# K blocks of 3, 3, 3, 3 and 4 chunks instead of four of 4 in the first layer's input projection

## The chip, the cores and the metric

The kernel runs on one core of one Trainium2 chip. The metric is the device time of one execution in microseconds, the median of three runs.

## The reference

A decoder trunk of two layers on 256 tokens of width 2048. Each layer has a mixer and a gated feed-forward part, each behind an RMS norm whose scale and shift come from a conditioning vector `c`. Cut to what the change touches:

```python
c_act = jax.nn.silu(c)
for l in range(DEPTH):
    mod = c_act @ w_mod[l] + b_mod[l]
    shift1, scale1, gate1, shift2, scale2, gate2 = jnp.split(mod[:, None, :], 6, axis=-1)
    h = rms_norm(x, norm1_gain[l]) * (1.0 + scale1) + shift1
    x = x + gate1 * hybrid_token_mixer(h, ...)      # proj = h @ w_in[l], then three mixers, then @ w_out[l]
    h = rms_norm(x, norm2_gain[l]) * (1.0 + scale2) + shift2
    x = x + gate2 * swiglu_ffn(h, ...)
return rms_norm(x, final_norm_gain)
```

All is float32. `w_mod[l]` is 2048 x 12288, and most of `w_in[l]` (3336 columns of it) is multiplied in the stage that the change touches.

## The kernel before, in words

**Engines.** TensorE (PE) does the products, VectorE (DVE) and ScalarE (ACT) the work around them, GpSimd (POOL) small fills, and the SyncE queue (SP) issues all transfers in order. A scheduler lays out each engine's order at build time from the order in which the code is written and from its own idea of durations; at run time every engine goes through its list in order.

**Modulation.** `mod = c_act @ w_mod` is done on DVE, not on PE. `mod_segment(l, part, k0, nk)` makes the `nk` chunks (128 columns each) from `k0` on of one part. A chunk row of `w_mod` comes in by DMA (L220) and L223 adds it, times one value of `c_act`, to an accumulator: 16 steps for the 16 chunks of `c`. Then `finish` transposes the accumulator on PE into the one `fin` bank (L248), DVE sums each column over the partitions (L250), and L253 (shift) or L256 (scale) writes the columns that the norm uses. In layer 0 a shift and a scale segment of a block run side by side, their steps in turn, in 128x512 buffers `g`.

**Pacing.** All steps stand in one list `mods`. The projection calls `tick` after each job, which pops steps at a rate; what is still missing when a norm asks for its columns is done there by `need`:

```python
rate[0] += rate[1] * weight          # weight: columns of the job / 1024
...
if mods and mods[0][0] not in closed:
    mods.popleft()[1]()
```

The rate is 3.3 in layer 0 and 1.6 in its last block. The segments of the gate and of the second norm are `closed` until the last block starts; their steps are 1024 wide, in two buffers `mraw`.

**The projection of layer 0.** It goes in K blocks. For each block, `norm` scales `x` (L441), transposes it (L444), applies scale and shift (L447 on ACT) and rounds (L450, L451); then four groups of columns are projected, "qk" (1024), "z" (520), "v" (768) and "bq" (1024). A job is one chunk of K of one group: a weight tile (L323), in one of nine buffers named `raw`, `wh` and `wl`, and float32 products (L358) with the two row blocks of 128 tokens into four `acc` banks. Behind the last job of a group the banks are evacuated: in the first block ACT copies them (L967), in the others DVE adds them to what stands there (L969). The normalised chunks lie in tiles of four chunks:

```python
j, i0 = divmod(at, 4)
n = min(4 - i0, ks[-1] + 1 - at)
if j not in res:
    res[j] = (tl_h32(), *(tl(hmp, [P, 4, P], "hm", F32R) for _ in range(2)))
```

Layer 1 takes all 16 chunks in one block, and the list of blocks is used nowhere else but here:

```python
for n in K_BLOCKS:
    for pair in zip(*(mod_segment(0, part, k0, n) for part in (SHIFT1, SCALE1))):
        mods.extend(pair)
    k0 += n
```

Of the kernel before, what the change touches and what calls it, by code (L numbers as in the profile page):

```python
# [33 lines left out]
FAR = 1.0e30  # L34


K_BLOCKS = (4, 4, 4, 4)
TAIL_OUT = (3, 6)
TAIL_FFN = (3, 5)
LEAD_FFN = (0, 0)  # L40
# [63 lines left out]
def trunk(ctx: ExitStack, tc, x, cT, pos, small, consts, b_mod, w_mod, w_in, w_gk, w_out,  # L104
# [369 lines left out]
    k0 = 0  # L474
    for n in K_BLOCKS:
        for pair in zip(*(mod_segment(0, part, k0, n) for part in (SHIFT1, SCALE1))):
# [472 lines left out]
    def layer(l):  # L949
        wi, wo = w_in[l], w_out[l]  # L950
        load_small(l)
        blocks, at = [], 0
        for n in (K_BLOCKS if l == 0 else (KD,)):
            blocks.append(range(at, at + n))
# [263 lines left out]
```

## Time and profile before

| | us |
|---|---|
| median of three runs | 2579.19 (2578.09 to 2586.53) |
| profiled execution | 2585.34 |
| its span, first to last instruction | 2583.5 |
| PE busy in the span | 2432.7 |
| DVE busy in the span | 1714.4 |
| first L358 matmul starts | 40.83 |
| layer 0's first norm has its columns | 40.19 |

Rows of the profile give an engine, a line, what is written from what, shapes and a count. In the order of time the first two columns are the start and the length in us, and a bracket at the end tells how long the engine stood idle ahead of the row and whose end it waited for. PE's ends are modelled, and merged rows overlap a little at their ends.

### The profile page before, as it was taken

How to read it: one execution, taken by the hardware profiler on the slowest of the kernel's cores; microseconds unless marked ns; L12 is line 12 of the kernel's file. 1: busy time of each engine (PE TensorE's matmuls, PEld its weight loads, DVE VectorE, ACT ScalarE, POOL GpSimd, SP SyncE). 2: the span in 40 equal slices, each digit the busy share in tenths (PEclk: the TensorE clock that was granted, in tenths of full speed). 3: DMA queues.
4: the chain of work that ended last, by engine and by line, in shares of the span. 5: the costliest groups of instructions: out<-in, count | busy, mean ns of one | idle time of the engine just before them, and what ended most of it. 6: DMA issues, size and time to landing. Idle time of an engine off the chain costs nothing.

```text
span 2583.5 us, 30803 instructions
## 1 busy us (share of the span) xinstructions
PE 2432.7 (94%) x11164; PEld 1884.1 (73%) x11164; DVE 1714.4 (66%) x2171; ACT 1053.5 (41%) x1548; POOL 58.2 (2%) x117
## 2 busy tenths in 40 slices
PE   4999998889999988999999999999999999999998
PEld 2555785447878767788877878877778878888876
DVE  6767867576675777657578785888664575544555
ACT  2203443124444333344335454564644434344443
POOL 1000000000000000000000000000000000000000
PEclk9999999989999999999999999999999999999999
DMA  9996538777778888868687861675676686666654
GB/s 341 368 322 204 180 114 282 258 231 268 261 259 260 283 268 274 292 193 286 223 277 261 281 192 50 214 232 192 212 256 193 200 286 195 188 191 188 189 184 155
DMA packets 190033, 600.79 MB, mean 233 GB/s; under 512 B 21628, under 2 KB 26268, under 8 KB 189496
## 3 DMA queue, kind: packets, MB, share of 16 engines
q1 hardware_dynamic: 189880, 598.81, 70.7%
q8 instruction: 88, 1.44, 0.2%
q14 instruction: 65, 0.53, 0.1%
HBM read 596.63 MB, written 2.10 MB: 232 GB/s over the span
## 4 chain that ended last, share of the span: by engine, by line
PE 57%; DMA 20%; DVE 10%; issue 8%; ACT 4%; POOL 1%; SPq 1%; DVEq 0%; ACTq 0%; POOLq 0%
PE acc L358 48%; DMA mraw<-in_w_mod 13%; DVE wl L331 4%; DMA raw<-in_w_down 3%; DMA raw<-in_w_in 2%; DVE acc L223 2%; ACT wh L330 1%; PE mm L403 1%; PE ga L895 1%; DMA raw<-in_w_up 1%; PE mm L678 1%; PE mm L685 1%; PE ga L916 1%; DMA raw<-in_w_gate 1%; PE fin L248 1%
## 5 line engine op out<-in xcount | busy, mean ns | idle before, releaser
L358 PE MATMUL acc<-wh,hm 128*128 128x512 f32 (+3 forms) x4872 | 1339.2, 389 | 20.9 <-DVE xs L931 4.7
L330 ACT ACTIVATE wh<-raw 128x1024 fp32r<-128x1024 f32 (+3 forms) x669 | 684.7, 1025 | 985.8 <-PE acc L358 548.9
L331 DVE TENSOR_TENSOR wl<-raw,wh 128x1024 fp32r<-128x1024 f32 (+3 forms) x669 | 785.2, 1179 | 446.6 <-ACT wh L330 444.5
L358 PEld LDWEIGHTS acc<-wh,hm 128*128 128x128 f32 x4872 | 892.0, 189 | 215.8 <-issue 25.5
L358 PE MATMUL acc<-wl,hm 128*128 128x512 f32 (+3 forms) x2484 | 792.3, 394 | 12.2 <-DVE wl L331 9.7
L223 DVE SCALAR_TENSOR_TENSOR acc<-mraw,c_act,acc 128x1024 f32<-128x1024 f32 x320 | 410.3, 1282 | 225.2 <-DMA mraw<-in_w_mod 222.9
L358 PEld LDWEIGHTS acc<-wl,hm 128*128 128x128 f32 x2484 | 458.4, 190 | 124.1 <-DVE wl L331 22.3
L358 PE MATMUL acc<-wh,ahl 128*128 128x512 f32 x560 | 158.4, 397 | 0.0
L358 PEld LDWEIGHTS acc<-wh,ahl 128*128 128x128 f32 x560 | 105.8, 189 | 24.5
L358 PE MATMUL acc<-wl,ahl 128*128 128x512 f32 x280 | 90.8, 398 | 7.2 <-DVE wl L331 7.2
L223 DVE SCALAR_TENSOR_TENSOR g<-g,c_act,g 128x512 f32<-128x512 f32 x128 | 88.7, 747 | 12.6 <-DMA g<-in_w_mod 12.4
L358 PE MATMUL acc<-wh,b 128*128 128x512 f32 (+2 forms) x184 | 74.7, 545 | 2.2 <-ACT b L447 2.1
L358 PE MATMUL acc<-wl,b 128*128 128x512 f32 (+2 forms) x176 | 67.1, 518 | 2.6 <-DVE g L969 2.6
L358 PEld LDWEIGHTS acc<-wl,ahl 128*128 128x128 f32 x280 | 52.2, 189 | 23.1 <-DVE wl L331 11.3
L358 PE MATMUL acc<-raw,b 128*128 128x512 f32 (+2 forms) x176 | 67.6, 524 | 0.0
L358 PEld LDWEIGHTS acc<-wh,b 128*128 128x128 f32 x184 | 35.2, 197 | 30.8 <-issue 23.1
L358 PEld LDWEIGHTS acc<-wl,b 128*128 128x128 f32 x176 | 32.8, 192 | 29.2 <-issue 20.3
L416 ACT ACTIVATE acc<-xs 128x512 f32<-128x512 f32 x32 | 19.0, 595 | 85.7 <-DVE xs L931 85.7
L447 ACT ACTIVATE b<-mm,mod,mod 128x128 f32<-128x128 f32 x24 | 9.2, 461 | 109.7 <-DVE mod L256 92.1
L358 PEld LDWEIGHTS acc<-raw,b 128*128 128x128 f32 x176 | 33.5, 195 | 26.7 <-issue 21.7
L929 DVE TENSOR_TENSOR acc<-acc,gate 128x512 f32<-128x512 f32 x64 | 43.0, 695 | 10.3 <-PE acc L358 10.2
L358 PE MATMUL acc<-raw,hm 128*128 128x512 f32 x88 | 41.7, 598 | 1.4 <-ACT acc L416 1.4
(314 smaller groups left out, 1645.8 us busy)
## 6 DMA issues: line engine op xcount, KB each, us to landing
mraw<-in_w_mod SPq DMA_DIRECT2D x320, 512.0 KB
raw<-in_w_down SPq DMA_DIRECT2D x176, 512.0 KB
raw<-in_w_gate SPq DMA_DIRECT2D x160, 512.0 KB
raw<-in_w_up SPq DMA_DIRECT2D x160, 512.0 KB
raw<-in_w_in SPq DMA_DIRECT2D x72, 512.0 KB
g<-in_w_mod SPq DMA_DIRECT2D x128, 256.0 KB
raw<-in_w_out SPq DMA_DIRECT2D x43, 512.0 KB
raw<-in_w_in SPq DMA_DIRECT2D x32, 264.0 KB
```

Of the source, the lines that this page charges most:

```text
L223: V.scalar_tensor_tensor(acc, raw[:, a], c_act[:, i + a:i + a + 1], acc, ALU.mult, ALU.add)
L248: TE.transpose(ps[:, i * P:(i + 1) * P], acc[:, (j + i) * P:(j + i + 1) * P], ident)
L330: A.activation(wh[:, :width], raw[:, :width], AF.Copy)
L331: V.tensor_tensor(wl[:, :width], raw[:, :width], wh[:, :width].bitcast(F32), ALU.subtract)
L358: TE.matmul(ps[blk, j][:, :segs[j][2]], xa, parts[j][part], start=i == 0 and n == 0, stop=last and n == len(terms) - 1)
L403: TE.transpose(ps[:, j * P:(j + 1) * P], src[:, j * P:(j + 1) * P], ident)
L416: A.activation(scr[0]() if junk is None else junk, xs[:, blk, j * 512:(j + 1) * 512], AF.Square, accum_out=ssq[blk][:, j:j + 1])
L678: TE.matmul(ps[:, s], LT[blk][:, s], Tm[blk][:, s], start=True, stop=True)
L685: TE.matmul(ps[:, s], U[blk][:, s], m1[:, s], start=True, stop=True)
L895: TE.matmul(ps[:, j * nk:(j + 1) * nk], qT[rows, i + j], kT[rows, g, :nk], start=True, stop=True)
L916: TE.matmul(ps[:, j * 64:(j + 1) * 64], pT[:, j * nk + kb * P:j * nk + (kb + 1) * P], kv[kb][:, P + g * 64:P + (g + 1) * 64], start=kb == ...
L929: V.tensor_tensor(ps, ps, need(gate_row, (l, part, j)), ALU.mult)
```

## The change

```diff
-K_BLOCKS = (4, 4, 4, 4)
+K_BLOCKS = (3, 3, 3, 3, 4)
```

Blocks now start at chunks 0, 3, 6, 9 and 12. The first four pairs of segments are 384 columns wide instead of 512, and there are 160 steps of them in all instead of 128. A block that does not start at a multiple of four is normalised in up to two pieces, so the norm runs in 7 pieces for each row block instead of 4. There is one more round of evacuations.

The rate of steps stays as it is: 3.3 times 3.258 (the columns of one chunk over 1024) is 10.75 steps for a chunk, 43 for a block of four and 32.25 for a block of three; each next pair of segments has 32 steps.

PE at the end of the first block, before: the last jobs of "bq" (`acc_560` to `acc_565`), the finish of the next block's two segments (`fin`), a transpose of the norm, and the second block's first job (`acc_690` on).

```order
L358 MATMUL acc_565<-wl_583,b_331 128x512
L248 MATMUL fin_640<-consts_88,g_357 128x128 x4
L358 MATMUL acc_560<-raw_601,b_195 128x512
L358 MATMUL acc_565<-raw_601,b_331 128x512
L248 MATMUL fin_649<-consts_88,g_363 128x128 x4
L358 MATMUL acc_560<-wh_616,b_195 128x512
L358 MATMUL acc_565<-wh_616,b_331 128x512
L444 MATMUL mm_677<-consts_88,b_675 128x128 x4
L358 MATMUL acc_690<-wl_688,b_656 128x512
```

(The two middle matmuls of each job are left out.) The same place now:

```order
L358 MATMUL acc_518<-raw_546,b_327 128x512
L358 MATMUL acc_519<-raw_546,b_327 128x512
L248 MATMUL fin_574<-consts_88,g_351 128x128 x3
L248 MATMUL fin_582<-consts_88,g_357 128x128 x3
L358 MATMUL acc_624<-wh_622,b_195 128x512
L444 MATMUL mm_605<-consts_88,b_603 128x128
L444 MATMUL ga_615<-consts_88,b_613 128x128 x2
L358 MATMUL acc_625<-wh_622,b_195 128x512
L358 MATMUL acc_628<-wh_622,b_327 128x512
```

Both `fin` groups have moved from between the last jobs of a block to behind its last matmul, and the next block's first matmul follows them.

DVE at the end of the second block, before: the evacuations of "bq" (L969) among steps of the fourth block's segments; the third block's columns were written some 25 rows earlier.

```order
L223 SCALAR_TENSOR_TENSOR g_828<-g_963,c_act_102,g_828 128x512
L969 TENSOR_TENSOR b_151<-b_151,acc_885 128x512
L969 TENSOR_TENSOR b_153<-b_153,acc_886 128x512
L969 TENSOR_TENSOR b_163<-b_163,acc_889 128x512
L223 SCALAR_TENSOR_TENSOR g_841<-g_966,c_act_102,g_841 128x512
L969 TENSOR_TENSOR b_165<-b_165,acc_890 128x512
L223 SCALAR_TENSOR_TENSOR g_828<-g_969,c_act_102,g_828 128x512
```

The same place now, with the third block's columns (`sums`, `mod`) behind the last evacuation and steps of the fourth block's segments (`g_897`, `g_903`) between them:

```order
L969 TENSOR_TENSOR b_163<-b_163,acc_783 128x512
L223 SCALAR_TENSOR_TENSOR g_897<-g_900,c_act_102,g_897 128x384
L969 TENSOR_TENSOR b_165<-b_165,acc_784 128x512
L250 TENSOR_REDUCE sums_251_839<-fin_840 128x3
L223 SCALAR_TENSOR_TENSOR g_903<-g_906,c_act_102,g_903 128x384
L253 COPY mod_6_3_250_838<-sums_251_839 128x3
L250 TENSOR_REDUCE sums_254_847<-fin_848 128x3
L223 SCALAR_TENSOR_TENSOR g_897<-g_909,c_act_102,g_897 128x384
L256 SCALAR_TENSOR_TENSOR mod_6_3_253_846<-sums_254_847,gains_131 128x3
```

What has moved is the finish of the next block's segments, from a place inside the block to its end. At the end of the fourth block, DVE's last step of the scale segment and a 1024-wide step of the gate stand there as well:

```order
L223 SCALAR_TENSOR_TENSOR g_1146<-g_1341,c_act_102,g_1146 128x512
L969 TENSOR_TENSOR b_165<-b_165,acc_1301 128x512
L223 SCALAR_TENSOR_TENSOR g_1152<-g_1344,c_act_102,g_1152 128x512
L250 TENSOR_REDUCE sums_408_1358<-fin_1359 128x4
L253 COPY mod_12_4_407_1357<-sums_408_1358 128x4
L250 TENSOR_REDUCE sums_411_1367<-fin_1368 128x4
L223 SCALAR_TENSOR_TENSOR acc_1407<-mraw_1410,c_act_102,acc_1407 128x1024
L256 SCALAR_TENSOR_TENSOR mod_12_4_410_1366<-sums_411_1367,gains_131 128x4
```

The gate's first step stood ahead of the last block's start by a group and more before (in row with the third block's "v" evacuations); it now stands in the finish itself.

## The prediction

> **What bounds the kernel now.** I read the page first, then busy time by stage, then the waits and the order of time of the first 220 us, where the change lies.
>
> ```profile
> span 2583.5 us, 30803 instructions
> PE 2432.7 (94%) x11164; PEld 1884.1 (73%) x11164; DVE 1714.4 (66%) x2171; ACT 1053.5 (41%) x1548; POOL 58.2 (2%) x117
> ```
>
> TensorE is busy 94% of the span. Busy time in two stretches (columns: stretch, length, then busy us of PE, PEld, DVE, ACT, POOL, then granted clock, DMA share, GB/s), and all that PE waited for from 84 to 198 us:
>
> ```profile
> 0.00:40.00 40.00, 3.35 (x12) 2.14 (x12) 26.74 (x57) 11.19 (x25) 6.59 (x27) 1.00 0.92 325
> 40.00:200.00 160.00, 157.31 (x468) 84.77 (x468) 109.50 (x175) 25.99 (x59) 2.73 (x16) 1.00 0.97 344
> PE fin L248 <- DVE sums L250: 0.8, 1, 0.8
> ```
>
> So there are 40 us in which PE has next to nothing, then 160 us in which it is the bound, although DMA is at 0.97 too. The three old block borders lie in the second stretch: the second block's last group gives way to the third's first at 138.59 us, and the third's ends with transposes at 184.59, both without a wait:
>
> ```profile
> 138.59 3.67 PE L358 MATMUL acc<-raw,b 128*128 128x512 f32 x8
> 184.59 0.60 PE L444 MATMUL mm<-consts,b 128*128 128x128 f32 x4
> ```
>
> A chunk of K is thus (184.59 - 138.59) / 4 = 11.5 us of PE. What the change can win is in the first 40 us, and what it can lose is at the borders. Order of time at the start, DVE then PE:
>
> ```profile
> 26.89 9.56 DVE L223 SCALAR_TENSOR_TENSOR g<-g,c_act,g 128x512 f32<-128x512 f32 x14 [0.38 <-DMA g<-in_w_mod]
> 36.88 0.69 DVE L250 TENSOR_REDUCE sums<-fin 128x4 f32<-128x512 f32 x1 [0.42 <-PE fin L248]
> 38.78 0.69 DVE L250 TENSOR_REDUCE sums<-fin 128x4 f32<-128x512 f32 x1 [1.00 <-PE fin L248]
> 39.38 0.74 DVE L223 SCALAR_TENSOR_TENSOR g<-g,c_act,g 128x512 f32<-128x512 f32 x1
> 40.04 0.15 DVE L256 SCALAR_TENSOR_TENSOR mod<-sums,gains 128x4 f32<-128x4 f32 x1
> ...
> 35.72 1.12 PE L248 MATMUL fin<-consts,g 128*128 128x128 f32 x4 [16.02 <-DVE g L223]
> 37.62 1.12 PE L248 MATMUL fin<-consts,g 128*128 128x128 f32 x4 [0.78 <-DVE sums L250]
> 40.83 2.08 PE L358 MATMUL acc<-wh,b 128*128 128x512 f32 x2 [2.09 <-ACT b L447]
> ```
>
> This is the finish chain of a modulation segment: transposes into the one `fin` bank, reduce, second transposes, second reduce, the scale column, ACT's L447, the first matmul. From the first `fin` at 35.72 to the matmul at 40.83 it takes 5.1 us. Its multiply-adds run back to back, 9.56 us for 14, 0.68 each: DVE sets the start, with DMA close behind (one 0.38 us gap).
>
> **The change part by part. The start.** A multiply-add on 384 instead of 512 columns is priced from two widths, and DMA's pace from the busiest row:
>
> ```profile
> L223 DVE SCALAR_TENSOR_TENSOR g<-g,c_act,g 128x512 f32<-128x512 f32 x60 | 41.7, 745 | 3.6 <-DMA g<-in_w_mod 3.6
> L223 DVE SCALAR_TENSOR_TENSOR acc<-mraw,c_act,acc 128x1024 f32<-128x1024 f32 x11 | 14.1, 1283 | 12.2 <-DMA mraw<-in_w_mod 12.2
> ...
> 20.00:40.00 20.00, 2.23 (x8) 1.43 (x8) 18.13 (x28) 0.00 (x0) 1.05 (x2) 1.00 1.00 361
> ```
>
> (1283 - 745) / 512 = 1.05 ns a column, so 128 columns fewer save 0.134 us, and the 32 of the first block 4.3 us. The chain loses two transposes (0.28 each, from 1.12 for four) and two times 0.13 of reduce, 0.8 together. The next transposes now stand ahead of the first matmul instead of behind it, worth nothing either way, and the slow first matmuls (2.08 for two) stay. Sum: -5.1. Lower bound -4 (DMA becomes the limit with its shorter rows), upper -7 (DMA sheds 2.1 MB, 5.8 us at 361 GB/s of the 20 to 40 us row, and DVE's gaps go too).
>
> **The borders.** A block needs 32 multiply-add steps for the next block's columns. The pace is 3.3 steps per 1024 columns of projection, 10.75 a chunk. Four chunks gave 43, so steps ran ahead; three give 32.25, so a block's last step now stands at the very end of the block before it. The order on PE shows it: before, both `fin` groups stand inside the last output group, ahead of its last jobs; now they stand behind its last matmul, at all four borders, and the next matmul needs their columns. So the finish chain, hidden until now behind bq matmuls, is exposed four times. How it ran when covered, and how DVE drains a group (PE, then DVE, near a border):
>
> ```profile
> 86.14 0.60 PE L248 MATMUL fin<-consts,g 128*128 128x128 f32 x4
> 86.58 3.60 PE L358 MATMUL acc<-wh,b 128*128 128x512 f32 x8
> 90.45 3.60 PE L358 MATMUL acc<-wl,b 128*128 128x512 f32 x8
> ...
> 137.93 0.69 DVE L969 TENSOR_TENSOR b<-b,acc 128x512 f32<-128x512 f32 x1 [0.17 <-PE acc L358]
> 138.53 0.74 DVE L223 SCALAR_TENSOR_TENSOR g<-g,c_act,g 128x512 f32<-128x512 f32 x1
> 139.19 0.68 DVE L969 TENSOR_TENSOR b<-b,acc 128x512 f32<-128x512 f32 x1
> ```
>
> I lay out each border from T, the end of the last bq matmul, with these pitches: `fin` of three warm 0.4, reduce 0.55, evacuation 0.6, multiply-add 0.54 (384) or 0.68 (512), scale column to first matmul 0.8 (40.04 to 40.83).
> - First border (the old block's evacuations are ACT's): fin 0.5, reduce to 1.1, fin and a multiply-add to 1.75, reduce to 2.3, matmul at 3.1.
> - Second: the last evacuation waits behind a multiply-add and ends at 0.95; reduce 1.5, multiply-add 2.0, second reduce 2.65, multiply-add 3.2, matmul at 4.0.
> - Third: the same with 512-wide multiply-adds: 4.6.
> - Fourth: the last scale step itself stands behind the last evacuation (1.75), two 4-wide reduces to 3.6, then a 1024-wide multiply-add (1.2) ahead of the column: 5.6.
>
> Together 17.3 us. PE does 39 transposes in there (0.11 each, from 0.43 for four) that it did elsewhere before: 4.3. Net +13.0; between 11 (multiply-adds between the reduces slip) and 15 (0.1 us more for each hand-over).
>
> **The clock.** What a stall of that size does afterwards is seen at 199 us, when PE waited for an evacuation:
>
> ```profile
> 201.50 2.20 PE L358 MATMUL acc<-wl,b 128*128 128x260 f32 x6 [2.58 <-DVE g L969]
> 206.10 1.19 PE L358 MATMUL acc<-raw,b 128*128 128x260 f32 x4
> ...
> 199.00:200.00 1.00, 0.00 (x0) 0.00 (x0) 0.43 (x1) 0.00 (x0) 0.00 (x0) 1.00 0.83 291
> 203.00:204.00 1.00, 1.00 (x4) 0.74 (x3) 1.00 (x2) 0.00 (x0) 0.00 (x0) 0.50 0.98 389
> 205.00:206.00 1.00, 1.00 (x4) 0.81 (x3) 0.92 (x1) 0.00 (x0) 0.00 (x0) 0.50 1.04 348
> 206.00:207.00 1.00, 1.00 (x5) 0.82 (x5) 0.37 (x1) 0.00 (x0) 0.00 (x0) 0.81 0.94 377
> ```
>
> 2.58 us of idling, and the granted clock stood at 0.50 from 203 to about 206.2 us: 3.2 us at half speed, 1.6 lost. A 0.78 us wait at 115 us did not lower it:
>
> ```profile
> 115.74 0.55 PE L248 MATMUL fin<-consts,g 128*128 128x128 f32 x3 [0.78 <-DVE sums L250]
> 116.00:117.00 1.00, 1.00 (x6) 0.52 (x5) 1.00 (x4) 0.00 (x0) 0.00 (x0) 1.00 1.07 403
> ```
>
> Idle time without the transposes is 2.4, 3.0, 2.8 and 4.7 us at the four borders, so each is nearer to the first case: four times 1.6, less a little chance of escape, +6. Ends: 1.6 (only the fourth) and 8.
>
> [...]
>
> **The last block.** The gate stream's first step and its nineteenth, and DVE's load behind them:
>
> ```profile
> 170.54 1.28 DVE L223 SCALAR_TENSOR_TENSOR acc<-mraw,c_act,acc 128x1024 f32<-128x1024 f32 x1
> 223.50 1.28 DVE L223 SCALAR_TENSOR_TENSOR acc<-mraw,c_act,acc 128x1024 f32<-128x1024 f32 x1
> ...
> 220.00:240.00 20.00, 19.94 (x65) 9.87 (x64) 19.55 (x50) 9.90 (x16) 1.16 (x2) 1.00 0.68 242
> ```
>
> Before, its first evacuations stood behind the eleventh step of the gate stream, which began at 170.5 us, 14 us ahead of the block; that made the 2.58 us stall and its 1.6 to 2 us of slow clock. Now the stream begins at the border and the evacuations stand behind its sixth step. The steps came one per 2.9 us (18 intervals from 170.54 to 223.50), so the sixth ends near T + 4.8 + 5 x 2.9 = 19.3; the evacuation is wanted near T + 18.4 (5.6, four jobs of 3.44, 1.6 of slow clock, less the last 2.6). I take half of the old 4.6 us as won back: -2.3 (0 to -4.6).
>
> Five stream steps are thereby pushed to DVE behind the block, 5 x 1.28 = 6.4 us, into a stage where DVE has little room (19.55 of 20 us busy); by the first attention scores the count is level again (22 before, 23 now). I take +2 (0 to 6.4).
>
> **At nothing.** One more block brings DVE a round of accumulating evacuations (about 8 us), 32 more multiply-add starts (4.5) and six more norm pieces (1.6); the cover is DVE's idle time, 160 - 109.5 = 50 us. If it goes, evacuations come late and PE waits for its four banks. SP issues 32 more transfers and two more bias rows, 11 us of a queue that mostly waits; bytes are the same. POOL's two memsets and ACT's smaller roundings lie beside PE. The matmuls are the same in number and kind. Behind 400 us the order on every engine is nearly unchanged, and the chain of waits leads through PE there, so a delay is handed on.
>
> Sum: -5.1 + 13.0 + 6 - 2.3 + 2 = +13.6 us. The profiled execution took 2585.3 with what lies around its span, so 2599 on its scale; it was slower than the median, 2579.2, and on that the forecast is 2593.
>
> **The rivals.** Faster: the chain at the borders fits under the last bq jobs, as it did at 82 to 90 us. It decides where the net bubble falls below 5.1 / 4 = 1.3 us a border. For it speaks only that the columns' data will mostly be there in time; against it, that PE takes its `fin` in order behind the last matmul, and the chain alone is 3 us. Time: -5.1 - 2.3, about 2572.
>
> Same (the wait is that at the second norm):
>
> ```profile
> 517.08 1.09 PE L248 MATMUL fin<-consts,acc 128*128 128x128 f32 x4 [5.88 <-DVE acc L223]
> ```
>
> Bubbles near their low end, clock kept, stall of the last block gone, or this 5.88 us wait taking some of it up: +2 to +7, about 2584. Against that, the steps that it waits for follow PE's own pace and come later too.
>
> Clock falls at the fourth border only: +9.2, 2588.
>
> Late transfers: the first border is short of data. SP's issues of the first block's pieces:
>
> ```profile
> 5.32 26.05 SPq L220 DMA_DIRECT2D g<-in_w_mod  x31
> ```
>
> Until it, DMA must bring 32 pieces of 196 KB, 1 MB of masks and 5.1 MB of weights, 12.4 MB, 34 us at 361 GB/s. SP was through with the first block's pieces at 31.4 us and will be some 4 us sooner: done near 62, with the border at 36 + 3 x 11.5 and the slow start, 73. If shorter rows cost 20% or the queue is held by full buffers, each border waits some us longer and evacuations behind such a step too: +18 to +26, about 2600.
>
> **How the numbers follow.** Forecast 0.50, clock at one border only 0.17, late transfers 0.12, same 0.15, faster 0.06. A measurement of this kernel tells 0.3%, 7.7 us, from no change. Slower by more: 0.46 of the 0.50, 0.14 of the 0.17 and all 0.12, 0.72. Within: 0.22. Faster: 0.06. The range takes the low ends (-7 + 11 + 1.6 - 4.6 + 0, +1) nearly, and the high ones (-4 + 15 + 8 + 0 + 6.4, +25): 2582 to 2604.
>
> **What the new profile would show.** First L358 matmul near 36 us (wrong if after 38). Four waits of PE at `fin` or at the first L358 of a block, 2 to 5 us each, on DVE's L223, L250 or ACT's L447, near 73, 112, 152 and 192 us, each followed by a clock of 0.50 in a 1 us row (wrong if there are none, or if the waits are for DMA). End of the bq group of the last block some 13 us later than before. The forecast fails if the first border shows under 1.5 us of idle PE.

## The result and the profile after

| | us |
|---|---|
| changed kernel, median of 4 runs | 2599.72 (2598.79 to 2604.76) |
| kernel before beside it, median of 4 runs | 2578.64 (2576.07 to 2586.53) |
| ratio, 95% interval | 1.0068 (1.0042 to 1.0095) |
| its profiled execution, and span | 2599.53, 2597.5 |

The change costs 0.68%, some 18 us. It was forecast as slower, 2593 in a range of 2582 to 2604. The page after: PE does the same 11164 matmuls, DVE 66 instructions more.

```profile
PE 2440.8 (94%) x11164; PEld 1884.3 (73%) x11164; DVE 1728.2 (67%) x2237; ACT 1056.1 (41%) x1554; POOL 55.9 (2%) x119
```

The two stretches that the prediction opened with (stretch, length, busy us of PE, PEld, DVE, ACT, POOL, then granted clock, DMA share, GB/s):

```profile
0.00:40.00 40.00, 6.85 (x18) 3.65 (x19) 25.35 (x66) 14.44 (x33) 5.86 (x27) 1.00 0.90 302
40.00:200.00 160.00, 148.51 (x444) 80.74 (x443) 115.82 (x225) 23.73 (x57) 3.21 (x18) 0.98 0.91 311
```

PE does 3.5 us more work than before in the first stretch and 8.8 us less in the second. The start, in the order of time (DVE, then PE):

```profile
18.15 5.49 DVE L223 SCALAR_TENSOR_TENSOR g<-g,c_act,g 128x384 f32<-128x384 f32 x10
...
36.55 4.84 PE L358 MATMUL acc<-wh,b 128*128 128x512 f32 x8
41.23 3.60 PE L358 MATMUL acc<-wl,b 128*128 128x512 f32 x8
```

Ten multiply-adds of 384 columns take 5.49 us, 0.55 each against 0.68. The first product begins at 36.55 instead of 40.83 us, 4.3 us earlier, and the second job at 41.23 instead of 47.33: a head start of 6.1 us. Then the four borders on PE:

```profile
72.87 0.55 PE L248 MATMUL fin<-consts,g 128*128 128x128 f32 x3 [0.65 <-DVE sums L250]
74.78 1.12 PE L358 MATMUL acc<-wh,b 128*128 128x512 f32 x2 [1.37 <-ACT b L447]
...
110.51 0.55 PE L248 MATMUL fin<-consts,g 128*128 128x128 f32 x3 [0.86 <-DVE sums L250]
112.86 1.13 PE L358 MATMUL acc<-wh,b 128*128 128x512 f32 x2 [1.80 <-ACT b L447]
...
148.98 0.55 PE L248 MATMUL fin<-consts,g 128*128 128x128 f32 x3 [0.49 <-DVE sums L250]
151.46 5.40 PE L358 MATMUL acc<-wh,b 128*128 128x512 f32 x8 [1.93 <-ACT b L447]
...
187.60 0.66 PE L248 MATMUL fin<-consts,g 128*128 128x128 f32 x4 [0.58 <-DVE g L223]
189.47 0.66 PE L248 MATMUL fin<-consts,g 128*128 128x128 f32 x4 [1.21 <-DVE sums L250]
192.72 2.07 PE L358 MATMUL acc<-wh,b 128*128 128x512 f32 x2 [2.60 <-ACT b L447]
```

From the end of the last bq matmul (71.73, 108.83, 146.91, and 186.86 from 183.42 and the 3.44 us of a job) to the next block's first product it is 3.05, 4.03, 4.55 and 5.86 us, 17.5 together. The releasers are the links of the finish chain in its order: reduce, second reduce, ACT's shift and scale.

How late the same matmul is in the trace after, along the span:

| matmul | before | after | difference |
|---|---|---|---|
| second job of the first block | 47.33 | 41.23 | -6.1 |
| first job of the last block | 185.03 | 192.72 | +7.7 |
| last product of the projection | 256.85 | 264.81 | +8.0 |
| L812, as the output projection begins | 457.39 | 467.64 | +10.2 |
| a transpose of L403 there | 475.30 | 487.79 | +12.5 |
| finish ahead of the second norm | 517.08 | 526.84 | +9.8 |
| last L823, in layer 1 | 1747.7 | 1757.5 | +9.8 |
| end of the span | 2583.5 | 2597.5 | +14.0 |

Two places behind the projection need a word. In the output projection the clock falls in after and not in before, behind the same instruction. The order of time of before, then of after, then a 5 us row of after:

```profile
457.39 0.68 PE L812 MATMUL mm<-a 64*128 64x128 f32 x4 [1.14 <-DVE a L804]
```

```profile
467.64 0.68 PE L812 MATMUL mm<-a 64*128 64x128 f32 x4 [1.56 <-DVE a L804]
```

```profile
470.00:475.00 5.00, 5.00 (x13) 2.62 (x11) 2.72 (x3) 0.38 (x1) 0.00 (x0) 0.50 0.87 294
```

A wait of 1.56 us in place of 1.14, and five microseconds at a clock of 0.50 behind it, where before stays at 1.00. At the second norm, on the other hand, part of the delay disappears:

```profile
526.84 0.81 PE L248 MATMUL fin<-consts,acc 128*128 128x128 f32 x4 [2.92 <-issue]
```

Before, PE waited 5.88 us there for a multiply-add of DVE, which ended at 516.93. Now the profile names no releaser, but the same multiply-add ends at 526.73, 0.1 us ahead of the row. That is 9.8 us later than before; PE came to the row 12.7 us later, with four products moved behind it, and the wait is 2.92.

### The profile page after: what moved, and what is told of

Same layout as the page of the kernel before. It is cut to its first block, busy times and chain, and to the rows that moved or that the text cites. A ratio compares the mean times of both kernels' runs of the same rounds, so it can differ in the third digit from the quotient of the medians.

```text
span 2597.5 us, 30989 instructions
## 1 busy us (share of the span) xinstructions
PE 2440.8 (94%) x11164; PEld 1884.3 (73%) x11164; DVE 1728.2 (67%) x2237; ACT 1056.1 (41%) x1554; POOL 55.9 (2%) x119
## 4 chain that ended last, share of the span: by engine, by line
PE 43%; DMA 18%; DVE 8%; issue 5%; ACT 3%; SPq 1%; POOL 0%; ACTq 0%; DVEq 0%; POOLq 0%
PE acc L358 38%; DMA mraw<-in_w_mod 12%; DVE wl L331 4%; DMA raw<-in_w_down 2%; DMA raw<-in_w_in 2%; DVE acc L223 2%; ACT wh L330 1%; DMA raw<-in_w_gate 1%; DMA raw<-in_w_up 1%; PE mm L403 1%; PE ga L895 0%; SPq L323 0%; DVE acc L929 0%; DMA raw<-in_w_out 0%; PE mm L685 0%
## 5 line engine op out<-in xcount | busy, mean ns | idle before, releaser
L358 PE MATMUL acc<-wh,hm 128*128 128x512 f32 (+3 forms) x4872 | 1339.3, 389 | 21.6 <-ACT acc L416 6.1
L358 PEld LDWEIGHTS acc<-wh,hm 128*128 128x128 f32 x4872 | 890.4, 189 | 216.3 <-issue 23.9
L358 PE MATMUL acc<-wl,hm 128*128 128x512 f32 (+3 forms) x2484 | 793.4, 394 | 16.5 <-DVE wl L331 11.3
L358 PEld LDWEIGHTS acc<-wl,hm 128*128 128x128 f32 x2484 | 457.7, 189 | 129.2 <-DVE wl L331 23.5
L358 PE MATMUL acc<-wh,ahl 128*128 128x512 f32 x560 | 160.0, 400 | 0.0
L358 PEld LDWEIGHTS acc<-wh,ahl 128*128 128x128 f32 x560 | 106.6, 191 | 25.4
L223 DVE SCALAR_TENSOR_TENSOR g<-g,c_act,g 128x384 f32<-128x384 f32 (+1 forms) x160 | 94.0, 640 | 9.7 <-DMA g<-in_w_mod 9.4
L358 PE MATMUL acc<-wl,ahl 128*128 128x512 f32 x280 | 92.0, 403 | 5.1 <-DVE wl L331 5.1
L358 PE MATMUL acc<-wh,b 128*128 128x512 f32 (+2 forms) x184 | 76.0, 551 | 7.9 <-ACT b L447 7.7
L358 PE MATMUL acc<-raw,b 128*128 128x512 f32 (+2 forms) x176 | 66.9, 518 | 1.7 <-DMA raw<-in_w_in 0.8
L358 PEld LDWEIGHTS acc<-wl,ahl 128*128 128x128 f32 x280 | 52.6, 191 | 21.5 <-DVE wl L331 9.4
L358 PE MATMUL acc<-wl,b 128*128 128x512 f32 (+2 forms) x176 | 66.1, 513 | 1.1 <-DMA wl<-in_w_in 0.7
L358 PEld LDWEIGHTS acc<-wh,b 128*128 128x128 f32 x184 | 35.2, 199 | 37.7 <-issue 20.3
L447 ACT ACTIVATE b<-mm,mod,mod 128x128 f32<-128x128 f32 x24 | 9.6, 455 | 128.1 <-DVE mod L256 126.7
L358 PEld LDWEIGHTS acc<-raw,b 128*128 128x128 f32 x176 | 33.0, 190 | 29.9 <-issue 23.2
L358 PEld LDWEIGHTS acc<-wl,b 128*128 128x128 f32 x176 | 32.9, 190 | 27.2 <-issue 22.2
L358 PE MATMUL acc<-raw,hm 128*128 128x512 f32 x88 | 43.5, 622 | 2.8 <-ACT acc L416 2.8
```

The lines of the kernel that those rows point to most:

```text
L223: V.scalar_tensor_tensor(acc, raw[:, a], c_act[:, i + a:i + a + 1], acc, ALU.mult, ALU.add)
L358: TE.matmul(ps[blk, j][:, :segs[j][2]], xa, parts[j][part], start=i == 0 and n == 0, stop=last and n == len(terms) - 1)
L447: A.activation(h32[:, i], ps[:, i * P:(i + 1) * P], AF.Identity, scale=mod_col[l, 3 * sub + 1, at + i], bias=mod_col[l, 3 * sub, at + i])
```

## The experiments

Each kernel is timed against the kernel before on its own chip (2581.35, 2582.17 and 2582.89 us in the three groups), and the ratio with its interval is what counts: one profiled execution can lie 13 us from its kernel's median, so traces are read here for places, not for totals. "The rate" is the first number of RATE_IN.

**The rate raised in five blocks.**

```diff
-RATE_IN = (3.3, 0.8)
+RATE_IN = (4.4, 0.8)
```

> The blocks of 3, 3, 3, 3, 4, but the pace of modulation steps in layer 0 raised from 3.3 to 4.4, so that a block of three chunks again pops 43 steps for the 32 that the next block needs. My theory (the steps run dry, so the finish chain is exposed at the block borders): the head start of about 6 us stays, the second to fourth border show no wait of TensorE at the fin transposes, the first still shows half a chain (the scale half, about 2 us); the time is 3 to 9 us under the kernel before, 2570 to 2576. Rival, five blocks as such (one more round of evacuations, more norm pieces on VectorE): the time stays 12 to 20 us over the kernel before. Rival, rows of 384 columns make the transfers slower: it stays over as well, and TensorE waits for DMA.

Measured: 2592.48 us, ratio 1.0041 (1.0024 to 1.0059). A miss: faster than the change by some 7 us, but not faster than before. What PE waited for between 30 and 275 us, the change first, then rate 4.4 (us in total, times, longest; the rows of the finish chain, of the norm's input and of transfers, and one more for DVE):

```profile
PE acc L358 <- ACT b L447: 7.7, 4, 2.6
PE fin L248 <- DVE sums L250: 3.9, 5, 1.2
PE mm L444 <- DVE b L441: 1.6, 1, 1.6
PE acc L358 <- DMA raw<-in_w_in: 0.8, 1, 0.8
PE acc L358 <- DMA wl<-in_w_in: 0.7, 2, 0.5
PE acc L358 <- DMA wh<-in_w_in: 0.2, 1, 0.2
```

```profile
PE mm L444 <- DVE b L441: 3.0, 3, 1.6
PE fin L248 <- DVE sums L250: 2.7, 3, 1.2
PE acc L358 <- DMA wh<-in_w_in: 2.3, 2, 1.6
PE acc L358 <- DVE g L223: 2.0, 1, 2.0
PE acc L358 <- DMA wl<-in_w_in: 1.4, 1, 1.4
PE acc L358 <- ACT b L447: 1.3, 1, 1.3
PE acc L358 <- DMA raw<-in_w_in: 1.1, 2, 0.6
```

The waits in the finish chain shrink from 11.6 to 4.0 us (0.65 and 0.80 us of them lie ahead of the first block, not at a border). In their place PE waits 4.8 us for weights, where it was 1.7, 3.0 for the norm's input, where it was 1.6, and once 2.0 for DVE, at 147.5 us inside the third block; the job behind that wait took 5.20 us to the next one's start instead of 3.43.

**A rate between.** The same edit with 3.7.

> The blocks of 3, 3, 3, 3, 4 with a pace of 3.7: 36 steps a block for the 32 needed, so the lead grows by four steps a block. My theory: chains partly exposed, 1 to 4 us of wait a border, 6 to 9 us in all instead of the changed kernel's 17.5 us from last bq matmul to next L358; the time lies between the changed kernel and the pace of 4.4, within 5 us of the kernel before. Rivals (five blocks, shorter rows): no difference to the changed kernel.

Measured: 2592.66, ratio 1.0045 (1.0028 to 1.0062): 12 us above before, where 5 were expected, and no different from 4.4. The third border is covered; the others stay open:

```profile
73.31 1.12 PE L358 MATMUL acc<-wh,b 128*128 128x512 f32 x2 [1.34 <-ACT b L447]
111.84 1.13 PE L358 MATMUL acc<-wh,b 128*128 128x512 f32 x2 [2.46 <-ACT b L447]
188.91 2.07 PE L358 MATMUL acc<-wh,b 128*128 128x512 f32 x2 [3.70 <-ACT b L447]
```

The last waits of the second and the fourth are longer than in the change (1.80 and 2.60), but part of the chain now lies inside the block: from the last bq matmul to the next product it is 1.8, 2.6 and 4.3 us, 8.7 together, where 6 to 9 were expected and the change has 17.5. So the borders came out as the theory has them and the time did not. Against the trace of before, this one is 4.0 us late as the projection ends (216 to 222 us) and 13 us late at 440 to 456 us: most of its loss arises behind the projection, where the rate of its blocks is no longer at work. Why was not tried.

**Four blocks, run dry.** The kernel before, with a rate at which a block of 4 pops just the 32 steps that are needed.

```diff
-RATE_IN = (3.3, 0.8)
+RATE_IN = (2.46, 0.8)
```

> Four blocks of four as before, but the pace lowered from 3.3 to 2.46, so that a block pops 32.06 steps for the 32 needed. My theory: all three borders now show the whole finish chain, 4 to 6 us each from the last bq matmul to the next L358, without any head start; 9 to 17 us over the kernel before. Rival, five blocks as such, and rival, shorter rows: nothing of theirs is in this kernel, so no change (within 4 us).

Measured: 2601.08, ratio 1.0076 (1.0048 to 1.0103), 20 us, a little above what was expected. Its three borders (from the last bq matmul to the next product 3.6, 4.4 and 5.2 us, 13 together; the other 7 us are not assigned):

```profile
91.24 1.85 PE L358 MATMUL acc<-wl,b 128*128 128x512 f32 x2 [1.52 <-ACT b L447]
142.66 2.07 PE L358 MATMUL acc<-raw,b 128*128 128x512 f32 x2 [1.53 <-ACT b L447]
194.91 2.08 PE L358 MATMUL acc<-wh,b 128*128 128x512 f32 x2 [2.08 <-ACT b L447]
```

The loss and the signature of the change come without five blocks. The ratio of steps popped to steps needed opens a border; a fifth block is not needed for it.

**Four blocks at the raised rate.** The kernel before with rate 4.4.

> The kernel before (four blocks of 4), rate 4.4 instead of 3.3. It tells what the raised rate costs by itself. Theory (the transfers bound the projection; slices asked for earlier push the weights behind them on the one in-order queue): PE gets waits for wh, wl or raw in the second to fourth block, and the time is 3 to 12 us above before, 2584 to 2593: then the +11 of the five blocks at 4.4 is mostly the rate. Rival (the rate is free, the +11 belongs to five blocks): within 3 us of before, 2578 to 2584.

Measured: 2597.68, ratio 1.0046 (1.0022 to 1.0071), at the upper end of what was expected. The raised rate costs four blocks some 12 us by itself, as much as five blocks at 4.4 are above before. In its trace between 30 and 275 us, where before has no wait for a transfer in this list, there are 9.4 us:

```profile
PE acc L358 <- DMA wh<-in_w_in: 5.3, 4, 4.0
PE acc L358 <- DMA wl<-in_w_in: 2.7, 3, 1.0
PE acc L358 <- DMA raw<-in_w_in: 1.4, 3, 1.0
```

**Half the slices left out.** Four kernels, five or four blocks at rate 3.3 or 4.4, in which a multiply-add with an odd index uses the slice that is already there:

```diff
-            raw = scr[1]() if early else tl(modp, [P, 1024], "mraw")
+            if early and i % 2:
+                raw = st["raw"]
+            else:
+                raw = scr[1]() if early else tl(modp, [P, 1024], "mraw")
...
+                st["raw"] = raw
```

Line numbers are four higher in these kernels: L362, L451, L252 and L254 are L358, L447, L248 and L250. Five blocks at 4.4, four at 3.3:

> The changed kernel (3, 3, 3, 3, 4) at rate 4.4, but every second row of the modulation slices of layer 0's shift 1 and scale 1 is not loaded: the step uses the slice before it again, so half of these 33.6 MB stays out of the queues, and the values of the modulation are others. DVE's and PE's work is that of the kernel at rate 4.4 (2592.5). Theory (the transfers bound the projection: DMA 0.91 busy over the first 250 us, so raising the rate takes the queues from the weights): without half the slices the waits of PE for wh, wl and raw between 60 and 165 us go, the first product starts between 24 and 32 us instead of 36, and the time falls by 10 to 25 us, to 2568 to 2582; and it is then 2 to 8 us below the four-block kernel with the same omission, as the shorter head and the covered borders promise. Rival (the price is in the five blocks themselves, the extra round of evacuations and the 32 more steps on DVE, not in transfers): it stays 5 to 15 us above the four-block kernel with the same omission.

> The kernel before (four blocks of 4, rate 3.3) with the same omission: every second row of the slices of shift 1 and scale 1 of layer 0 is not loaded, the step uses the slice before it again. It is the mate of the five-block kernel with half the slices. If the transfers bound the first 40 us, the first product starts near 30 to 34 us instead of 40.8 (32 multiply-adds of 0.67 us are 21.5 us on DVE, from about 8 us on), and the time is 6 to 15 us below before, 2566 to 2575. If DVE and not the transfers set the start, it begins within 3 us of 40.8 and the time is within 4 us of before.

Five at 3.3, four at 4.4:

> Five blocks (3, 3, 3, 3, 4) with every second row of the slices of shift 1 and scale 1 not loaded, as in the kernel that took 2572.0, but at the rate 3.3 of the change instead of 4.4. Theory (the borders of the change are a chain of DVE, PE and ACT behind the last step of the segments, and the rate alone decides whether it lies inside the block; transfers have no part in it): the four exposed chains come back in full, PE waits for b L451 and sums L254 behind every block, and the time rises by 8 to 16 us, to 2580 to 2588. Rival (the steps at the borders are late because their slices land late): with half the slices the chains stay covered at 3.3 too, and the time is within 4 us of 2572.

> Four blocks of 4 with the same omission, at rate 4.4 instead of 3.3. With all slices the rate 4.4 cost some 12 to 15 us in four blocks (2597.7 against 2582.2). Theory (that cost is transfers: slices asked for earlier stand ahead of the weights on the one queue): with half the slices it is gone, and the time is within 5 us of the 2583.0 of the rate 3.3, or up to 8 us below; the 11 us between the two kernels with half the slices then belong to the five blocks with covered borders. Rival (the cost is DVE's: more steps ahead of the evacuations and the norm): it stays, 2591 to 2599.

Measured (us, ratio to before with its interval), beside the kernels with all slices:

| | four blocks | five blocks |
|---|---|---|
| all slices, rate 3.3 | 1 (before) | 2599.72, 1.0068 (1.0042 to 1.0095) |
| all slices, rate 4.4 | 2597.68, 1.0046 (1.0022 to 1.0071) | 2592.48, 1.0041 (1.0024 to 1.0059) |
| half, rate 3.3 | 2583.00, 1.0003 (0.9985 to 1.0021) | 2587.24, 1.0026 (1.0010 to 1.0042) |
| half, rate 4.4 | 2570.76, 0.9958 (0.9945 to 0.9972) | 2571.99, 0.9955 (0.9936 to 0.9974) |

Half the slices at 3.3 gained nothing in four blocks: there the queue keeps up, and the first product starts at 39.1 us instead of 40.8, so DVE sets the start. With five blocks and half the slices it starts at 33.8 us, where 24 to 32 was expected. At 4.4 half the slices gain 0.9% in each kind of block: what the raised rate costs is transfers. (Between the rates in four blocks I had expected no gain above 8 us; it was 12, and why the raise gains that much once the slices are halved was not tried.) I first took the 11 us between the five-block kernel at 4.4 and the four-block kernel at 3.3 for a gain of the five blocks, and the table takes that back: at 4.4 the two columns are level, with all slices and with half. The short head is used up by what a fifth block brings. At 3.3 the fifth block costs 17.5 us with all slices and 6 with half (0.0068 and 0.0023 of 2582; by the two intervals the 6 may be anything from 0 to 12).

The border chains do not come from late slices: at 3.3 with half of these transfers they are all there. PE's waits from 30 to 275 us, five blocks at 3.3 and then at 4.4:

```profile
PE acc L362 <- ACT b L451: 10.6, 5, 4.4
PE fin L252 <- DVE sums L254: 6.3, 5, 1.7
```

```profile
PE acc L362 <- ACT b L451: 4.0, 2, 2.1
PE fin L252 <- DVE sums L254: 1.6, 2, 1.2
```

That the fifth block costs less with half the slices has a trace of a cause at the second norm. There, four blocks at 3.3 wait 5.5 us for DVE's multiply-add and five blocks at 3.3 wait 2.5 us; a lag of the second against the first of 9.1 us ahead of that wait (485 to 510 us) is 5.2 us right behind it and 0.3 us at 640 us. It was not tried by itself, and stays open.

**The block of four at the front.** K_BLOCKS = (4, 3, 3, 3, 3), all else as in the change.

> Five blocks, but the block of four first (4, 3, 3, 3, 3), pace 3.3. The first block pops 43 steps, so the steps stay 11 ahead at every later border; no head start. By its order three borders are covered and the fourth is not (both fin groups behind the last matmul). My theory: the first L358 at about 41 us as before, one chain of 4 to 6 us at the last border, 2 to 8 us over the kernel before. Rival, five blocks as such: as slow as the changed kernel without its head start, 18 to 26 us over. Rival, shorter rows: 8 us over or more, with TensorE waiting for DMA.

Measured: 2612.74, ratio 1.0127 (1.0101 to 1.0153), a miss. Its last projection product is earlier than before's, 248.99 against 256.85, and only the fourth border shows; it loses behind the projection. So the next kernel changed the rate in the last block alone:

```diff
-RATE_LAST = 1.6
+RATE_LAST = 2.1
```

> The kernel (4, 3, 3, 3, 3), which took 2612.7, with the rate in the last block at 2.1 instead of 1.6. Theory on its loss: its projection ended 8 us earlier than before's, but the steps of gate 1, shift 2 and scale 2 are closed until the last block, and a last block of 3 chunks at rate 1.6 pops 15.6 of them where a block of 4 pops 20.9; the rest come late at the second norm (PE waited 10.6 us for a step of the accumulator there, and the next product was 24 us behind before's). At 2.1 the block of 3 pops 20.5: the wait at the second norm falls to 3 to 7 us and the time by 8 to 18 us, to 2595 to 2605. Rival (the loss is the last block's place or the fourth border, not the number of steps): within 4 us of 2612.7.

Measured: 2592.57, ratio 1.0046 (1.0026 to 1.0066): 20 us back from that one number, where 8 to 18 were expected. PE's waits at the second norm, 480 to 620 us, at 1.6 and at 2.1:

```profile
PE fin L248 <- DVE acc L223: 10.6, 1, 10.6
```

```profile
PE fin L248 <- DVE sums L250: 4.1, 1, 4.1
PE fin L248 <- DVE acc L223: 2.6, 1, 2.6
```

A last block of three chunks popped too few steps of gate 1, shift 2 and scale 2. This wait alone shrinks by 4 us only; with all of PE's waits in the stretch it is 28.6 against 15.2 us, and at 640 to 700 us the same matmuls are 17 us earlier. (The profiled execution at 2.1 loses most of that lead again later and ends 13 us above its kernel's median.) The last block's length is a budget for what comes behind it, which the prediction did not need for (3, 3, 3, 3, 4), since its last block keeps four chunks.

**More steps in the last block of before.** Four blocks, RATE_LAST = 2.0.

> The kernel before (four blocks of 4) with the rate of the last block at 2.0 instead of 1.6. The block (4, 3, 3, 3, 3) gained 20 us from 2.1, since a last block of 3 popped too few steps of gate 1, shift 2 and scale 2. Before's own last block pops 20.9 and still leaves a wait of 5.9 us at the second norm. If that wait is a shortage of steps: 26 popped, the wait falls under 2 us and the time by 3 to 6 us, to 2576 to 2579. If the steps that are pulled into the last block push its own evacuations and the GDN work on DVE instead: within 3 us of before or up to 8 us slower.

Measured: 2583.68, ratio 0.9993 (0.9977 to 1.0010), no change. The wait at the second norm went from the steps to a later link, the residual of DVE:

```profile
PE acc L358 <- DVE xs L931: 6.2, 1, 6.2
```

**Three chunks first, four later.** The low rate and the opening of the gate from the fourth block on.

```diff
-K_BLOCKS = (3, 3, 3, 3, 4)
+K_BLOCKS = (3, 4, 4, 4, 1)
-            rate[1] = RATE_LAST if last and l == 0 else RATE_IN[l]
-            if last:
+            rate[1] = RATE_LAST if l == 0 and bi >= 3 else RATE_IN[l]
+            if last or bi == 3:
```

> Blocks of 3, 4, 4, 4 and 1 chunks; the lower rate 1.6 and the opening of gate 1, shift 2 and scale 2 from the fourth block on instead of the fifth (20.9 steps popped there, 8 of them for the last chunk, and 5.2 in the last block: 18 of the 48 against 20.9 before). A kernel meant to keep the short head and lose only one border. Theory: first product near 36 us (5 to 6 us won); the first border is exposed (32.25 steps popped, 32 needed, now 512 wide) for 3 to 5 us, the second and third are covered as before (43 against 32), the fourth too (8 steps needed); one extra round of evacuations on DVE in the one-chunk block, where PE has only 9.8 us of products, for 0 to 6 us; the stream 3 steps short, 0 to 8 us. Sum -3 to +14: 2579 to 2596. Rival (each block more costs 6 us or over at its border whatever the rate, as if it were the block and not the chain): 2596 to 2610.

Measured: 2589.28, ratio 1.0023 (1.0009 to 1.0037), inside what was expected: the best five-block kernel with all slices, and still 6 us above before. Its first product starts at 35.37 us. Between 30 and 275 us its PE waits 6.7 us for weights, where before shows no such wait; that is as much as the loss, but was not taken out by itself. The one exposed border:

```profile
75.95 1.12 PE L358 MATMUL acc<-wh,b 128*128 128x512 f32 x2 [1.53 <-ACT b L447]
```

No kernel that does the whole computation beat the kernel before.

## Why the prediction was right, and where it was not

| term of the sum | predicted | in the trace after |
|---|---|---|
| start | -5.1 (-7 to -4) | -6.1 |
| borders | 17.3, net +13.0 | 17.5, net +13.2 |
| clock at the borders | +6 (1.6 to 8) | +3.5 |
| last block | -2.3 (-4.6 to 0) | -1.9 (second job +9.9, end +8.0) |
| stage behind it | +2 (0 to 6.4) | +2.2 up to L812 |
| further on | handed on unchanged | +2.3, -2.7, 0, +4.2 |
| sum | +13.6 | +14.7 by the rows above; +14.2 by the times (2599.53 - 2585.34) |

(The rows leave out 0.7 us that PE won between the borders: the first three terms end at +9.9 at the second job of the last block, where -6.1, +13.2 and +3.5 make +10.6.)

**The start was right, but not in all its parts.** The first product came 4.3 us earlier, which is the 5.1 less the transposes that now stand ahead of it. The slow first matmuls were to stay, and became fewer: the first job takes 4.68 us to the second one's start, against 6.50 less 0.85 of transposes before, 1.0 us shorter.

**The borders were right in kind and size**, chain by chain: 3.1, 4.0, 4.6 and 5.6 predicted, 3.05, 4.03, 4.55 and 5.86 measured. The four-block kernel run dry and the half-slice kernel at 3.3 confirm that the rate against the need opens them, and that neither a fifth block nor late slices are needed for it.

**The clock was over-sized.** It was laid on all four borders, because each stall was near the 2.58 us of the one example. It fell behind the third and fourth only, and why two borders kept their clock no run shows. Granted clock behind the second, third and fourth:

```profile
114.00:115.00 1.00, 1.00 (x5) 0.53 (x4) 1.00 (x4) 0.77 (x4) 0.00 (x0) 1.00 1.06 393
...
153.00:154.00 1.00, 1.00 (x3) 0.34 (x2) 0.46 (x1) 0.97 (x3) 0.00 (x0) 0.50 1.00 319
...
194.00:195.00 1.00, 1.00 (x3) 0.41 (x2) 0.59 (x1) 0.38 (x1) 0.00 (x0) 0.50 0.86 352
```

The first job of the third block takes 5.23 us to the second one's start where the first two after a border show 3.87 with three transposes between and a bare job takes 3.43; the fourth's takes 5.61. That is 1.8 and 1.7, 3.5 together. PE's idle time at the borders was 2.0, 2.7, 2.4 (in two pieces) and 4.4 us (in three pieces, the longest 2.60). The low end of 1.6 took the fourth border alone, where that time is longest; the clock fell at the third too, where it is shorter than at the second.

**The last block was right, its end was not.** The old 2.58 us stall is gone, with waits of 0.41 and 0.77 us for evacuations in its place, and between the second job and the end 1.9 us are won back. But the end was announced "some 13 us later" and came 8.0 later. The prediction's own terms up to there make 11.6, not 13, so 1.4 of the difference is in the announcement; of the other 3.6, 2.5 are the clock's, 1.0 the start's, and the rest small gains between the borders.

**What failed is "a delay is handed on".** The forecast of the total is near for a reason that it did not give, and in that it is luck. The delay grew by 2.3 us behind the half clock at 470 us, lost 2.7 at the second norm, and gained 4.2 in layer 1. The rival "same" named that 5.88 us wait as a cushion, and it was one, but a thin one: as the prediction had argued, the multiply-add that PE waits for came later too, by 9.8 us. In layer 1, one wait of PE for DVE (L1138) took 5.57 us at 2109 us instead of 2.71, behind a step of DVE that stood 4.11 us waiting for its slice of `w_mod`. The four-block kernel with RATE_LAST 2.0, which is no slower than before, has a step of the same kind there (+3.8 us against the one profiled execution of before), and in the thirteen traces beside before's, the change's among them, the step against before lies anywhere from 0.1 to 10 us. So I count that one to the execution and not to the change; this is argued and not tried. Without it the profiled sum would be near +10, and the medians say +18 to +21; where the rest of the medians' difference lies, one trace of each cannot tell.

**"At nothing" held only in part.** The extra evacuations and starts hid behind PE at 3.3. But five blocks at 4.4, with the borders mostly covered, are level with four at 4.4. Of the 6 us of the head start, the finish chains left in it take 1.7 (3.3 us of PE's waits behind the first product against 1.6 with four blocks); the rest is lost to something else that a fifth block brings, and no run tells whether to the evacuations, the smaller norm pieces or the rows of 1536 bytes.

**The rivals.** "Faster, 2572" needed the chain under the last bq jobs. At 4.4 most of it is there, and the time is 2592: covering the borders was not enough, since the rate that covers them takes the queue from the weights. "Late transfers" was wrong as a cause of the borders at 3.3 (1.7 us of waits for weights in the change, none of them at a border) and right as the price of a higher rate.

## What to carry to other kernels

When a loop is cut into smaller blocks and something is prepared one block ahead at a fixed rate, compare what a block pops with what the next one needs: 43 against 32 hid the finish chain, 32.25 against 32 exposed it at every border, about 4.4 us each here. Raising the rate is not free where the same queue brings the weights: 12 us in four blocks, gone when half of these transfers were left out. And look at what the last block supplies to the stages behind it: one chunk less there cost 20 us, which a rate of 2.1 instead of 1.6 gave back.

## What the runs showed of the hardware

In these traces the length of the idle time alone did not tell whether the clock fell. In the change, 2.7 us in two pieces at the second border left it at 1.00; 2.4 us in two pieces at the third was followed by 0.50 for 3.41 us (from 151.68 us), 4.4 us in three pieces at the fourth also by 0.50 for 3.41 us (from 192.64), and in the output projection a wait of 1.56 us by 0.50 for 6.83 us (from 469.12), where before waited 1.14 us and stayed at 1.00. PE's work just ahead did not tell it alone either. Busy time in 3.42 us with most of the second border in them, and in the 3.41 us ahead of the fall behind the third:

```profile
110.72:114.14 3.42, 1.62 (x8) 0.86 (x7) 3.31 (x10) 1.66 (x5) 0.00 (x0) 1.00 1.00 337
148.27:151.68 3.41, 0.99 (x6) 0.53 (x5) 3.41 (x9) 0.73 (x3) 0.00 (x0) 1.00 0.95 325
```

The 1.62 us of work was not followed by a fall and the 0.99 us was, but so was 1.85 us, in the 3.41 us ahead of 469.12. What decides was not shown. Of slow clock, the 2.0 and 2.7 us of idle time at the first two borders cost nothing, the 2.4 us at the third 1.8 us and the 4.4 us at the fourth 1.7.

Rows of 384 columns made the queues dearer by the byte. MB moved by the main queue in the first 250 us and its share of the 16 engines, before and after:

```profile
q1 hardware_dynamic: 35878, 79.64, 90.1%
```

```profile
q1 hardware_dynamic: 39663, 76.66, 90.3%
```

0.901 x 250 / 79.64 is 2.83 us for a MB before, and 0.903 x 250 / 76.66 is 2.94 after: 4% more, 9 us of queue time for those 77 MB. A median packet of 1536 bytes took 65 ns and one of 2048 bytes 84 ns, 3% more by the byte. DVE's own price came out as the widths promised: 0.55 us for 384 columns, 0.68 for 512.
